# Masked copies of K in halves, in a linear ReLU attention kernel

## The chip, the cores and the metric

One core of a Trainium2 chip. The metric is the device time of one execution in microseconds (us); the kernel before was timed three times, and the profile is of one more execution. TensorE multiplies matrices, VectorE, ScalarE and GpSimd (POOL in the profile) work element by element, SyncE (SP) only issues DMAs here. PE, DVE and ACT in the profile are TensorE, VectorE and ScalarE.

## The reference

```python
# Q, K, V: float32 of shape (8, 12, 512, 64): batch, heads, rows, dim
Q_feat = np.maximum(0, Q)
K_feat = np.maximum(0, K)
KV = np.einsum('bhkd,bhkv->bhdv', K_feat, V)
K_sum = np.sum(K_feat, axis=2)
numerator = np.einsum('bhqd,bhdv->bhqv', Q_feat, KV)
denominator = np.einsum('bhqd,bhd->bhq', Q_feat, K_sum)
return numerator / (denominator[:, :, :, None] + 1e-10)
```

Attention without a softmax: for each of the 96 heads a 64 x 64 product `KV` of K and V over the 512 rows is made first, and then each row of Q is multiplied with it and divided by its own sum.

## The kernel before

The 96 heads are worked on in 12 octets of 8 heads (NO = 12). An octet of Q, K or V is 128 partitions of 32 rows of 64 numbers; a head lies in 16 partitions. POOL loads them with DMAs that turn float32 into bf16 (`load_q`, line 174, and `load`, line 179); the K and V of octet 0 come as float32 over SP. Nine octets fit in the input buffers (NI = 9), so the loads run far ahead of the work.

All 64 partitions of four heads are multiplied in one matmul, so the heads have to be kept apart by zeros. VectorE therefore makes two masked copies of K, `kf[:, :, s, :]` for s = 0 and 1 (`prep_k`, line 189): relu of K, times a mask that keeps every second head. V has two masked copies in `vo` (`prep_v`, line 195), with a column of ones that gives `K_sum`.

The code runs in steps (`step`, line 313). Step i does the following on each engine, in this order:

- TensorE (`products`, line 350, a loop that waits on semaphores): transposes Q of octet i (line 360); makes KV in two groups of 64 matmuls in all, group 0 over rows 0 to 15 and group 1 over rows 16 to 31 of each partition, with a signal after each group (line 369); transposes the result of octet i-1 back to rows (line 378); multiplies Q with KV, first the denominators, then two halves of the numerators (all line 354, into `ps_kv` and `ps_x`).
- ScalarE: relu of the transposed Q (line 209), KV out of PSUM (line 217), half of a V copy for octet i+1 (line 200), the numerators out of PSUM (line 225).
- VectorE: a copy of Q of octet i+1 (`copy_q`, line 206), the two K copies of octet i+1 (line 191), two `norm`s of octet i-1 (numerator times reciprocal into the output buffer, line 242), three small instructions for the denominators of octet i (lines 230 to 237), and the rest of the V copies of octet i+1 (line 202).

The tile `kf` exists once. So the K copies of octet i+1 have to wait until TensorE has read those of octet i. The class `Order` (line 9) derives such waits from keys: each operation lists the keys it reads and writes, and it waits for the operations of other engines that last used them. The engines take their instructions strictly in the order written. TensorE's side is entered by `do.looped`, whose keys for the two KV groups are the lists `KF[0]` and `KF[1]` (line 257).

Three queues set the order of transfers. POOL's DMAs go over six semaphores in turn, so that each waits for the landing of the one six places before it; POOL also issues the stores of octets 0 and 1 (line 251). SP issues the stores of octets 2 to 11 (line 254), and each of them also waits for the K load of octet 11 to have landed. The output has seven buffers (NOUT = 7, two of which held octet 0's K and V first): octet o's `norm` writes buffer (o + 2) mod 7 and waits for the store of octet o-7.

Of the kernel before, what the change touches and what calls it, by code (L numbers as in the profile page):

```python
# [96 lines left out]
def kernel(  # L97
# [14 lines left out]
    R = S * 4 // P  # L112
# [24 lines left out]
    mask = sb.tile([P, 2, 2], fp32, name="mask")  # L137
    mask_h = sb.tile([P, 8, 2], fp32, name="mask_h")
    kf = sb.tile([P, RQ, 2, D], bf16, name="kf")
    vo = sb.tile([P, RQ, 2, D4], bf16, name="vo")  # L140
# [26 lines left out]
    do = Order(nc, sems)  # L167

    def kv_src(o):
        if o == 0:  # L170
            return (o_sb[0], ("o", 0)), (o_sb[1], ("o", 1))
        return [(x[o % NI].rearrange("p (r d) -> p r d", d=D), (n, o % NI)) for n, x in (("k", k_sb), ("v", v_sb))]
# [6 lines left out]
    def load(o):  # L179
        i = o % NI  # L180
        for n, X, t in (("K", Kr, k_sb), ("V", Vr, v_sb)):
            if n == "V" and o == NO - 1:
                load_q(o)
            do.op("pool", lambda e: e.dma_start(out=t[i], in_=X[o], single_packet=True), writes=[(n.lower(), i)],  # L184
                  dma=lane("pool"))
        if o < NO - 1:
            load_q(o)

    def prep_k(o, s):
        src, key = kv_src(o)[0]  # L190
        do.op("dve", lambda e: e.tensor_scalar(kf[:, :, s, :], src, scalar1=0.0, scalar2=mask[:, 0, s:s + 1],  # L191
                                               op0=Alu.max, op1=Alu.mult),
              reads=[key, ("mask", 0)], writes=[("kf", s)])

    def prep_v(o, t, halves, who, sem=None):
        src, key = kv_src(o)[1]
        rs = slice(R * halves[0], R * halves[-1] + R)
        to, src, m = vo[:, rs, t, 2:D + 2], src[:, rs], mask[:, 1, t:t + 1]
        if who == "act":
            make = lambda e: e.activation(to, src, Act.Copy, scale=m)  # L200
        else:
            make = lambda e: e.tensor_scalar(to, src, scalar1=m, scalar2=None, op0=Alu.mult)  # L202
        do.op(who, make, reads=[key, ("mask", 1), "vo1"], writes=[("vo", t, j) for j in halves], sem=sem)

    def copy_q(o):
        do.op("dve", lambda e: e.tensor_copy(q2, q_sb[o % NI]), reads=[("q", o % NI)], writes=["q2"], sem="q2")  # L206

    def relu_q(j):
        do.op("act", lambda e: e.activation(qt[:, j * (U // 2):(j + 1) * (U // 2)], ps_qt[j], Act.Relu),  # L209
              reads=[("pq", j)], writes=[("qt", j)])  # L210
# [3 lines left out]
    def evac_kv():  # L214
        for s in range(2):
            for c in range(2):
                do.op("act", lambda e: e.copy(  # L217
                    kvd[64 * c:64 * c + 64, s:8:2, c * D1:c * D1 + D1].rearrange("p (g t) d -> p g t d", t=2),
                    ps_kv[64 * s:64 * s + 64, :, 0:2 * (D + 2)].rearrange(
                        "p g (t d) -> p g t d", t=2)[:, :, :, c:c + D1]),  # L220
                    reads=[("pk", 0), ("pk", 1)], writes=[("kvd", s, c)], sem="ev" if s + c == 2 else None)

    def copy_ot(j, who):
        to, src = ot[:, :, 4 * j:4 * j + 4], ps_x[j].rearrange("p (h u c) -> p u h c", h=4, u=U)
        do.op(who, lambda e: e.copy(to, src) if who == "act" else e.tensor_copy(to, src),  # L225
              reads=[("x", j)], writes=[("ot", j)], sem=f"t{j}")

    def denominators():
        ps = ps_den.rearrange("p (u h c) -> p u (h c)", u=U, h=8)
        do.op("dve", lambda e: e.scalar_tensor_tensor(  # L230
            own.rearrange("p u h c -> p u (h c)"), ps, 1e-10,
            mask_h.rearrange("p h c -> p (h c)").unsqueeze(1).to_broadcast([P, U, 16]), op0=Alu.add, op1=Alu.mult),
            reads=["pd", "mask_h"], writes=["own"])
        do.op("dve", lambda e: e.tensor_reduce(  # L234
            out=den.rearrange("p (u c) -> p u c", c=2), in_=own.rearrange("p u h c -> p u c h"), op=Alu.add,
            axis=mybir.AxisListType.X), reads=["own"], writes=["den"])
        do.op("dve", lambda e: e.reciprocal(rec, den), reads=["den"], writes=["rec"])

    def norm(o, j):
        i = (o + 2) % NOUT  # L240
        rs = slice(16 * j, 16 * j + 16)
        do.op("dve", lambda e: e.tensor_tensor(o_sb[i][:, rs], ps_x[j].rearrange("p (r d) -> p r d", d=D),  # L242
                                               rec[:, rs].unsqueeze(2).to_broadcast([P, 16, D]), op=Alu.mult),
              reads=[("x", j), "rec"], writes=[("o", i, j)] if i > 1 else [("o", i, j), ("o", i)], sem=f"n{j}")

    def store(o):
        i = (o + 2) % NOUT
        to, src = Or[o], o_sb[i].rearrange("p r d -> p (r d)")
        keys = [("o", i, h) for h in range(2)]
        if o + AHEAD + 1 < NO:  # L250
            do.op("pool", lambda e: e.dma_start(out=to, in_=src, single_packet=True), reads=keys, dma=lane("pool"))
        else:
            keys.append(("k", (NO - 1) % NI))
            do.op("sp", lambda e: e.dma_start(out=to, in_=src), reads=keys,
                  dma=lane("sp" if o + NOUT < NO else "last"), kept=o + NOUT >= NO)

    KF = [[("kf", 0), ("kf", 1), ("vo", 0, j), ("vo", 1, j), "vo1"] for j in range(2)]
    PK = [("pk", 0), ("pk", 1)]
    QT = [("qt", 0), ("qt", 1)]
    OT = [("ot", 0), ("ot", 1)]  # L260
# [31 lines left out]
    def setup():  # L292
        do.op("dve", lambda e: e.tensor_copy(ident32, ident), reads=["ident"], writes=["ident32"])
        for c in range(2):
            do.op("dve", lambda e: e.tensor_reduce(
                out=mask_h[:, :, c], in_=ident32.rearrange("p (h b) -> p h b", h=8), op=Alu.add,
                axis=mybir.AxisListType.X), reads=["ident32"], writes=[("mh", c), "mask_h"])
        do.op("dve", lambda e: e.tensor_reduce(
            out=mask[:, 0, :], in_=mask_h[:, :, 0].rearrange("p (a s) -> p s a", s=2), op=Alu.add,
            axis=mybir.AxisListType.X), reads=["mask_h"], writes=[("mask", 0)])  # L300
        prep_k(0, 0)
        prep_k(0, 1)
        prep_v(0, 1, (0,), "act", "a0")
        prep_v(0, 0, (0, 1), "dve", "d0")
        prep_v(0, 1, (1,), "dve", "d1")
        do.op("dve", lambda e: e.memset(kvf.bitcast(fp32)[:, 0:4 * D1], 0.0), writes=KVD, sem="n0")
        do.op("dve", lambda e: e.memset(kvf.bitcast(fp32)[:, 4 * D1:], 0.0), writes=KVD, sem="n1")
        copy_q(0)
        for j in range(2):
            nc.scalar.sem_inc(sems[f"t{j}"], 1)  # L310
            do.note("act", "act", (), (), f"t{j}", 1)

    def step(i):
        r = i + 1
        more, last = i + 1 < NO, i == NO

        if not last:
            do.looped([("q2", r)], ["q2", "ident"], [("pq", 0)])
            do.looped([], ["q2", "ident"], [("pq", 1)])
            relu_q(0)  # L320
            relu_q(1)
            do.looped([("a0", r), ("d0", r)], KF[0], PK + ["pd"])
            do.looped([("d1", r)], KF[1], PK + ["pd"])
            evac_kv()
            if more:
                prep_v(i + 1, 1, (0,), "act", "a0")
                copy_q(i + 1)
                prep_k(i + 1, 0)
                prep_k(i + 1, 1)
        if i > 0:  # L330
            o = i - 1
            do.looped([("t0", r), ("t1", r)], [*OT, "ident32"], [("x", 0)])
            do.looped([], [*OT, "ident32"], [("x", 1)])
            for j in range(2):
                norm(o, j)
            store(o)
            if o + AHEAD + 1 < NO:
                load(o + AHEAD + 1)
        if not last:
            do.looped([("ev", r)], [*QT, *KVD], ["pd"])  # L340
            denominators()
            for j in range(2):
                do.looped([(f"n{j}", r)], [*QT, *KVD], [("x", j)])
            copy_ot(0, "act")
            copy_ot(1, "act" if more else "dve")
            if more:
                prep_v(i + 1, 0, (0, 1), "dve", "d0")
                prep_v(i + 1, 1, (1,), "dve", "d1")
# [85 lines left out]
```

## Time and profile before

| | us |
|---|---|
| three runs, median (lowest to highest) | 125.53 (125.38 to 125.61) |
| profiled execution | 125.56 |
| its span, first to last instruction | 123.7 |
| TensorE matmuls busy | 85.0 (69%) |
| VectorE busy | 82.4 (67%) |
| ScalarE busy | 78.3 (63%) |
| DMAs on the chain that ended last | 71% |
| VectorE's K copies of octets 1 to 11 (22) | 15.6, 0.75 each |

Spans and starts in the profile are counted from the first instruction; the execution's time has 1.86 us more than the span. "Idle before" in a profile line tells how long the engine stood still before the instruction, and the name behind the arrow what it waited for last. The granted clock is that of TensorE, 1.00 being full speed. The chain that ended last is found by going back from the last instruction to whatever released it. Two instructions of one engine can overlap at their ends, so a pair may take less than the sum of its two times.

### The profile page before, as it was taken

To read this page: it belongs to the slowest core of one execution; us is meant where nothing else is said; L and a number is where in the kernel's file an instruction comes from. 1 tells how busy PE (TensorE), PEld (TensorE's weight loads), DVE (VectorE), ACT (ScalarE), POOL (GpSimd) and SP (SyncE) were. 2 spreads that over 40 slices of the span, in tenths; PEclk is the share of its full clock that TensorE was granted. 3 is DMA by queue.
4 is the path that set the end of the run, shared out by engine and by line. 5 is a ranking of instruction groups with operands and counts; after the bars stand their busy time and mean duration, and the time that the engine had idled before them with its cause. 6 is when DMAs were issued, how large, how long until landed. Compare 5 with 4: busy or idle time off the path is not lost.

```text
span 123.7 us, 3402 instructions
## 1 busy us (share of the span) xinstructions
PE 85.0 (69%) x1440; PEld 73.5 (59%) x1440; DVE 82.4 (67%) x127; ACT 78.3 (63%) x108; POOL 27.6 (22%) x55
## 2 busy tenths in 40 slices
PE   0000097697896979969799697996978918983900
PEld 0000096686794867949589485794856916972900
DVE  1261904769789697895987959869688649067330
ACT  0000762998987889878898788987869736652000
POOL 5795311331131213312421142221000000000000
PEclk9999999999999999999999999999999996897555
DMA  3999999999999999999999999999999999999955
GB/s 69 404 315 222 213 215 212 212 212 212 216 215 215 212 212 212 217 215 213 213 215 212 212 212 267 334 215 234 354 217 212 404 424 432 421 421 429 434 238 212
DMA packets 6916, 32.55 MB, mean 263 GB/s; under 512 B 768, under 2 KB 768, under 8 KB 5120
## 3 DMA queue, kind: packets, MB, share of 16 engines
q0 software_dynamic: 5184, 19.93, 75.8%
q1 hardware_dynamic: 1728, 12.58, 24.7%
q14 instruction: 3, 0.02, 0.0%
q8 instruction: 1, 0.02, 0.0%
HBM read 37.75 MB, written 12.58 MB: 407 GB/s over the span
## 4 chain that ended last, share of the span: by engine, by line
DMA 71%; PE 8%; DVE 7%; issue 5%; POOL 4%; POOLq 0%; DVEq 0%; SPq 0%
DMA k_sb<-in_K_dram 54%; DMA q_sb<-in_Q_dram 12%; DMA out_dram<-o_sb 6%; DVE o_sb L242 5%; PE ps_x L378 4%; PE ps_kv L369 2%; POOL vo L263 2%; PE ps_qt L360 1%; DVE ot_sb L225 1%; PE ps_x L354 1%; POOL k_sb L184 1%; POOL mask L263 1%; POOL q_sb L175 1%; POOL v_sb L184 0%; DVE den L234 0%
## 5 line engine op out<-in xcount | busy, mean ns | idle before, releaser
L242 DVE TENSOR_TENSOR o_sb<-ps_x,rec 128x1024 f32<-128x1024 f32 x24 | 28.5, 1217 | 9.2 <-PE ps_x L378 6.6
L225 ACT COPY ot_sb<-ps_x 128x1024 f32<-128x1024 f32 x23 | 23.2, 1013 | 10.7 <-PE ps_x L354 9.8
L369 PE MATMUL ps_kv<-vo,kf 64*128 64x132 bf16 x768 | 26.7, 228 | 0.8 <-DVE vo L202 0.2
L378 PE MATMUL ps_x<-ident,ot_sb 128*128 128x128 f32 x192 | 25.3, 288 | 1.7 <-DVE ot_sb L225 1.7
L369 PEld LDWEIGHTS ps_kv<-vo,kf 64*128 64x128 bf16 x768 | 24.7, 99 | 2.6 <-issue 2.6
L360 PE MATMUL ps_qt<-ident,q 128*128 128x128 bf16 x192 | 14.4, 235 | 16.4 <-DVE q L206 15.4
L209 ACT ACTIVATE qt<-ps_qt 128x1024 bf16<-128x1024 bf16 x24 | 23.4, 1031 | 1.9 <-PE ps_qt L360 1.9
L378 PEld LDWEIGHTS ps_x<-ident,ot_sb 128*128 128x128 f32 x192 | 22.3, 148 | 3.2 <-issue 2.0
L360 PEld LDWEIGHTS ps_qt<-ident,q 128*128 128x128 bf16 x192 | 12.4, 106 | 19.0 <-DVE q L206 15.4
L217 ACT CAST kvd<-ps_kv 64x260 bf16<-64x260 f32 x48 | 17.9, 374 | 8.5 <-PE ps_kv L369 7.6
L354 PE MATMUL ps_x<-qt,kvd 128*128 128x256 bf16 x96 | 14.9, 281 | 12.1 <-DVE o_sb L242 12.0
L191 DVE TENSOR_SCALAR kf<-k_sb,mask 128x2048 bf16<-128x2048 bf16 x22 | 15.6, 750 | 8.5 <-PE ps_kv L369 8.4
L354 PEld LDWEIGHTS ps_x<-qt,kvd 128*128 128x128 bf16 x96 | 7.7, 100 | 16.9 <-DVE o_sb L242 16.3
L206 DVE COPY q<-q_sb 128x2048 bf16<-128x2048 bf16 x12 | 8.2, 686 | 8.6 <-DMA q_sb<-in_Q_dram 8.6
L175 POOL DMA_DIRECT2D q_sb<-in_Q_dram x12 | 9.2, 763 | 19.0 <-DMA q_sb<-in_Q_dram 14.6
L200 ACT ACTIVATE vo<-v_sb,mask 128x1024 bf16<-128x1024 bf16 x11 | 12.7, 1153 | 0.6 <-DMA v_sb<-in_V_dram 0.4
L202 DVE TENSOR_SCALAR vo<-v_sb,mask 128x2048 bf16<-128x2048 bf16 (+1 forms) x22 | 11.6, 568 | 0.0
L184 POOL DMA_DIRECT2D k_sb<-in_K_dram x11 | 7.7, 697 | 16.8 <-DMA k_sb<-in_K_dram 12.9
L184 POOL DMA_DIRECT2D v_sb<-in_V_dram x11 | 6.3, 576 | 16.5 <-DMA v_sb<-in_V_dram 12.7
L200 ACT ACT_TABLE_LOAD x1 | 1.3, 1283 | 12.2 <-DMA o_sb<-in_V_dram 12.2
L354 PE MATMUL ps_kv<-kvd,qt 128*128 128x16 bf16 x192 | 6.9, 179 | 1.7 <-ACT kvd L217 1.7
L354 PEld LDWEIGHTS ps_kv<-kvd,qt 128*128 128x128 bf16 x192 | 6.4, 96 | 2.0 <-ACT kvd L217 1.9
(21 smaller groups left out, 27.6 us busy)
## 6 DMA issues: line engine op xcount, KB each, us to landing
out_dram<-o_sb SPq DMA_DIRECT2D x10, 1024.0 KB, 12.4
q_sb<-in_Q_dram POOLq DMA_DIRECT2D x12, 512.0 KB, 14.5
k_sb<-in_K_dram POOLq DMA_DIRECT2D x11, 512.0 KB, 14.4
v_sb<-in_V_dram POOLq DMA_DIRECT2D x11, 512.0 KB, 14.4
out_dram<-o_sb POOLq DMA_DIRECT2D x2, 1024.0 KB, 14.7
o_sb<-in_K_dram SPq DMA_DIRECT2D x1, 1024.0 KB, 6.2
o_sb<-in_V_dram SPq DMA_DIRECT2D x1, 1024.0 KB, 10.7
```

What stands on the lines that cost most here:

```text
L184: do.op("pool", lambda e: e.dma_start(out=t[i], in_=X[o], single_packet=True), writes=[(n.lower(), i)], dma=lane("pool"))
L191: do.op("dve", lambda e: e.tensor_scalar(kf[:, :, s, :], src, scalar1=0.0, scalar2=mask[:, 0, s:s + 1], op0=Alu.max, op1=Alu.mult), reads= ...
L200: make = lambda e: e.activation(to, src, Act.Copy, scale=m)
L202: make = lambda e: e.tensor_scalar(to, src, scalar1=m, scalar2=None, op0=Alu.mult)
L209: do.op("act", lambda e: e.activation(qt[:, j * (U // 2):(j + 1) * (U // 2)], ps_qt[j], Act.Relu), reads=[("pq", j)], writes=[("qt", j)])
L217: do.op("act", lambda e: e.copy(kvd[64 * c:64 * c + 64, s:8:2, c * D1:c * D1 + D1].rearrange("p (g t) d -> p g t d", t=2), ps_kv[64 * s:64 ...
L225: do.op(who, lambda e: e.copy(to, src) if who == "act" else e.tensor_copy(to, src), reads=[("x", j)], writes=[("ot", j)], sem=f"t{j}")
L242: do.op("dve", lambda e: e.tensor_tensor(o_sb[i][:, rs], ps_x[j].rearrange("p (r d) -> p r d", d=D), rec[:, rs].unsqueeze(2).to_broadcast( ...
L354: return pe.matmul(out_, lhsT, rhs, start=True, stop=True, skip_group_check=True)
L360: x = pe.transpose(ps_qt[u // 8][:, u % 8, :], q2[:, u, :], ident)
L369: x = pe.matmul(ps_kv[:, h, 0:2 * (D + 2)].rearrange("p (t d) -> p t d", t=2), kf[ps, R * g + k, :, :].rearrange("p s d -> p (s d)"), vo[p ...
L378: x = pe.transpose(ps_x[u // 8][:, u % 8 * P:u % 8 * P + P], ot[:, u].rearrange("p h c -> p (h c)"), ident32)
```

## The change

`prep_k` gets a third argument, the halves of the rows that it copies, and writes one key for each half. The KV groups of TensorE read only their own half's keys. For octet 0 both halves are still copied by one instruction for each s. In the steps, the two instructions of 32 rows become four of 16 rows: first both masked copies of rows 0 to 15, which wait for TensorE's group 0 of the octet before, then both of rows 16 to 31, which wait for group 1. `copy_q` stays ahead of all four and the `norm`s stay behind them.

```diff
-    def prep_k(o, s):
+    def prep_k(o, s, halves):
         src, key = kv_src(o)[0]
-        do.op("dve", lambda e: e.tensor_scalar(kf[:, :, s, :], src, scalar1=0.0, scalar2=mask[:, 0, s:s + 1],
+        rs = slice(R * halves[0], R * halves[-1] + R)
+        do.op("dve", lambda e: e.tensor_scalar(kf[:, rs, s, :], src[:, rs], scalar1=0.0, scalar2=mask[:, 0, s:s + 1],
                                                op0=Alu.max, op1=Alu.mult),
-              reads=[key, ("mask", 0)], writes=[("kf", s)])
+              reads=[key, ("mask", 0)], writes=[("kf", s, j) for j in halves])
...
-    KF = [[("kf", 0), ("kf", 1), ("vo", 0, j), ("vo", 1, j), "vo1"] for j in range(2)]
+    KF = [[("kf", 0, j), ("kf", 1, j), ("vo", 0, j), ("vo", 1, j), "vo1"] for j in range(2)]
...
-        prep_k(0, 0)
-        prep_k(0, 1)
+        prep_k(0, 0, (0, 1))
+        prep_k(0, 1, (0, 1))
...
                 copy_q(i + 1)
-                prep_k(i + 1, 0)
-                prep_k(i + 1, 1)
+                for j in range(2):
+                    for s in range(2):
+                        prep_k(i + 1, s, (j,))
```

## The prediction

> **What bounds the kernel now.** I read the chain that ended last first, then the timeline around it, then the clock in stretches of 3.41 us. The chain (start, length, what):
>
> ```profile
> 63.69 14.43 DMA q_sb<-in_Q_dram
> ...
> 78.40 14.85 DMA k_sb<-in_K_dram
> ...
> 93.27 7.43 DMA out_dram<-o_sb
> ...
> 100.72 2.37 DVE o_sb L242 x2
> ...
> 117.68 1.23 DVE o_sb L242
> ```
>
> It goes over transfers until 100.70: each load waits for the one six places ahead of it, the K load of octet 11 lands at 93.25, the store of octet 2, which waits for that landing, ends 7.43 us after, and its end frees the output buffer of the `norm` of octet 9. From there engines carry the chain. The page's slice row has the DMA engines at 9 of 10 or more from the second slice to the thirty-eighth. What VectorE does before 100.72 matters only if it is late for one of these landings. So: how late is it?
>
> ```profile
> 71.45 2.07 PE L369 MATMUL ps_kv<-vo,kf 64*128 64x132 bf16 x64
> 71.62 0.69 DVE L206 COPY q<-q_sb 128x2048 bf16<-128x2048 bf16 x1
> ...
> 73.45 1.97 PE L378 MATMUL ps_x<-ident,ot_sb 128*128 128x128 f32 x16
> ...
> 73.56 1.42 DVE L191 TENSOR_SCALAR kf<-k_sb,mask 128x2048 bf16<-128x2048 bf16 x2 [1.25 <-PE ps_kv L369]
> 74.89 2.47 DVE L242 TENSOR_TENSOR o_sb<-ps_x,rec 128x1024 f32<-128x1024 f32 x2
> ...
> 88.42 0.69 DVE L206 COPY q<-q_sb 128x2048 bf16<-128x2048 bf16 x1 [1.23 <-DMA q_sb<-in_Q_dram]
> ...
> 90.84 2.36 DVE L242 TENSOR_TENSOR o_sb<-ps_x,rec 128x1024 f32<-128x1024 f32 x2 [0.37 <-DMA out_dram<-o_sb]
> ```
>
> The first five lines are an ordinary step (octet 8's KV product): the `kf` copies start 1.25 us late, 0.11 after the transpose back (L378) starts, since they wait for the second KV group, and the `norm` follows. The last two are where loads catch up: `copy_q` of octet 10 waits 1.23 us for Q, the `norm` of octet 8 waits 0.37 for the store of octet 1. One step later the `norm` of octet 9 waits 2.11:
>
> ```profile
> 100.72 2.35 DVE L242 TENSOR_TENSOR o_sb<-ps_x,rec 128x1024 f32<-128x1024 f32 x2 [2.11 <-DMA out_dram<-o_sb]
> ...
> 102.00 0.61 PE L354 MATMUL ps_x<-qt,kvd 128*128 128x256 bf16 x4 [2.54 <-DVE o_sb L242]
> ...
> 103.97 1.91 PE L360 MATMUL ps_qt<-ident,q 128*128 128x128 bf16 x16
> ...
> 105.81 2.30 PE L369 MATMUL ps_kv<-vo,kf 64*128 64x132 bf16 x64
> ```
>
> Those 2.11 us are the slack of everything ahead of it. Behind it TensorE is cold: L360 takes 1.91 here against 1.06 in an ordinary step. Stretches (us, PE, PEld, DVE, ACT, POOL busy, granted clock, DMA share, GB/s):
>
> ```profile
> 75.64:79.05 3.41, 2.30 (x32) 1.60 (x28) 3.31 (x7) 2.66 (x4) 1.18 (x2) 1.00 1.03 362
> ...
> 99.53:102.94 3.41, 0.61 (x4) 0.31 (x4) 2.22 (x2) 1.06 (x2) 0.00 (x0) 1.00 1.01 428
> 102.94:106.35 3.41, 3.21 (x32) 2.72 (x34) 2.21 (x6) 2.87 (x4) 0.00 (x0) 0.50 1.00 423
> 109.77:113.18 3.41, 1.88 (x27) 1.17 (x24) 3.34 (x6) 1.01 (x1) 0.00 (x0) 1.00 1.00 423
> ...
> 21.03:24.44 3.41, 1.82 (x34) 1.73 (x35) 2.51 (x6) 3.29 (x6) 0.68 (x2) 1.00 1.05 211
> ```
>
> TensorE had been idle 2.53 us (99.47 to 102.00); the clock falls to 0.50 at 102.94, returns at 106.35, 3.41 us on, and falls again at 113.18, 6.83 after that. So it steps on a grid of 3.41 us: a cell with 0.61 us of work and one with 1.88 are followed by a slow one, cells with 1.82 and 2.30 are not. The limit lies near 1.8.
>
> **The change, by parts.** The profiled execution took 125.56 us, 123.7 of it span and 1.86 around it; the median is 125.53.
>
> 1. *Two more VectorE instructions an octet.* No row shows a half K copy. Its nearest rows:
>
> ```profile
> L191 DVE TENSOR_SCALAR kf<-k_sb,mask 128x2048 bf16<-128x2048 bf16 x22 | 15.6, 750 | 8.5 <-PE ps_kv L369 8.4
> ...
> L202 DVE TENSOR_SCALAR vo<-v_sb,mask 128x2048 bf16<-128x2048 bf16 x11 | 7.2, 657 | 0.0
> ...
> L202 DVE TENSOR_SCALAR vo<-v_sb,mask 128x1024 bf16<-128x1024 bf16 x11 | 5.3, 478 | 0.0
> ```
>
> Half of V costs 0.478/0.657 = 0.73 of the whole; on K's 0.75 that is 0.55, and since two in a row overlap by 0.08 (a pair takes 1.42, not 1.50), 0.47 from start to start. Bounds: 0.34 (half of the whole's 0.67) and 0.67 (no cheaper). I take 0.47, by the V row, its likest. An octet's copies then cost 4 x 0.47 + 0.08 = 1.96 instead of 1.42: +0.54 us (bounds 0.02 and 1.34).
>
> 2. *The first pair moves forward.* Times from the start of L369: group 0 ends at +1.03, `copy_q` at +0.85, group 1 at +2.07. The first pair runs from +1.05 to +1.99, in the 1.25 us gap, which covers its 0.94. The second starts at +2.10 and lets the `norm` start at +3.04; today that is +3.44 (71.45 to 74.89). Next late is TensorE's L378: with VectorE waiting, the `norm` of octet 10 started 1.20 after L378 did (108.04 to 109.24), so +3.20. Gain 0.24 us a step, a period of 7.44 to 7.57 instead of 7.68 to 7.81. Even at 0.34 it stays 0.24; at 0.67 the `norm` starts at +1.05 + 4 x 0.67 = +3.73, 0.29 later than now.
>
> 3. *The new wait.* The first half waits for group 0. Behind it in VectorE's order stand the other halves, two `norm`s, three denominator instructions, the V copies; TensorE and ScalarE wait for the `norm`s. Group 0 ends a microsecond before group 1, so it holds nothing that did not wait longer before. Where Q comes late, all four halves follow `copy_q`: with `copy_q` w later than +0.16 the `norm` can start at +0.78 + w + 1.88, past +3.20 when w is over 0.54. Loads bring an octet in 7.36 us, so the faster loop runs into that and then goes at the loads' pace.
>
> 4. *Queues.* POOL's loads wait for landings (its wait rows name only DMAs and the start), K of octet 11 goes into a buffer read long before, SP's ten stores wait for the K landing. No DMA is added or moved.
>
> *Sum up to 100.72.* The loop is shorter from octet 4 on, so L369 of octet 9 starts about 0.9 to 1.7 us before its 86.94. There it ends: Q of octet 10 is still copied at 88.42. Four halves from 89.04 end at 90.92 plus a tail, so the `norm` of octet 8 starts at 90.92, not 90.84: +0.08 (0 at 0.34 each, +0.88 at 0.67). That is absorbed in 2.11. Gain at 100.72: zero.
>
> *What the early work does to the clock.* L378 of step 9 then ends near 89.2 to 90.0 and the small matmuls near 89.6 to 90.4, so TensorE idles 1.7 to 2.5 us until 92.1. The cell 89.29 to 92.70 holds some 0.9 to 1.7 us of work instead of 2.61, under the limit, so I expect a slow cell from 92.70 to 96.11 that the kernel lacks now. Its price, from the same instructions at 103 to 106: L354 1.04 for 0.61, L360 1.91 for 1.06; L369 of octet 10 starts 0.8 to 1.3 us after its 95.09. L378 then starts at 98.0 to 98.4, its first half is ready 1.20 later, at 99.2 to 99.6, and `kf` of octet 11 is done by 99.5: all before 100.72. Cover left is 1.1 us. The cell 99.53 to 102.94 then has 1.4 to 1.8 us of TensorE work in place of 0.61, still at or under the 1.88 that did not suffice, so it is followed by the same slow cell, and the tail is today's.
>
> Forecast: 125.56 + 0 = 125.56 for that execution, 125.5 for a median. Within 0.2% (0.25 us) is what a measurement here cannot tell from no change.
>
> The Trainium skill, TensorE: Matmul & The Clock Gate, "What's actually happening", says that the activity window is about 3.4 us, free-running, and not reset by a kernel's start. The grid of 3.41 us agrees. By it, the cells would lie elsewhere in another execution, and the faster rival below would come in some executions; four executions between 125.38 and 125.61 don't show such a spread.
>
> **Rivals.**
>
> *Faster: the tail stays warm.* If the work pushed behind 99.53 brings the cell over the limit, the slow cell at 102.94 goes. For it: 1.82 once sufficed and the estimate reaches 1.8. Against: 1.88 did not. Price: (1.04 - 0.61) + (1.91 - 1.06) + (2.30 - 2.07) = 1.51 us off the chain. The stores keep the DMA engines full until 118.2, and the last store moves its data from about 119.4, so only 1.2 comes out: 124.3.
>
> *Slower: VectorE's extra copies hold up POOL's descriptors.* POOL's DMA instructions take 0.53 us mostly, but 0.83 to 1.02 beside VectorE copies (1.02 at 48.92, ahead of a `copy_q` at 49.13). 22 more copies in other places can stretch more of them. Should each of the six reissues on the chain (14.54, 29.25, 44.03, 58.74, 63.69, 78.40) land 0.1 to 0.49 later, K of octet 11 is 0.6 to 2.9 late, and so is all behind it: 126.1 to 128.4, at the nearer end 126.1. Against: the reissues with 0.53 and with 0.93 landed alike in 14.43, since five more loads are under way. It decides once the DMA share falls below 1 between 16 and 93 us.
> The Trainium skill, SBUF — State Buffer, the warning on the "DVE blocks DMA" trap, speaks for this rival: a DMA issued from GpSimd has its descriptors written there, and a VectorE copy in a two-port mode locks it out. The long issues agree; that the engines then stand idle no row here shows.
>
> *Slower: halves as dear as wholes.* At 0.67 each the period grows by 0.29, the `norm` of octet 9 comes at about 100.7, just at its limit; at 0.75 without overlap it would be about 2 us late, less up to 1.51 for a warmer tail: 126.1. Against: the V row.
>
> *The change does not do what it says:* the halves still start after group 1. Then the `norm` starts at +2.10 + 1.88, 0.54 later each step: 3.2 over six steps and 1.1 over the next two, less the 0.46 that the `norm` of octet 8 has in hand (86.94 + 3.44 against 90.84) and the 2.11, so 1.75 late, less up to 1.51 for a warm tail: 125.8 to 127.3. Against: the key of each half is written apart, and group 0 signals by itself.
>
> **How the numbers follow.** Forecast 0.54 (within 0.2%). Warm tail 0.25 (faster). POOL's descriptors 0.13, dear halves 0.05, no overlap 0.03 (slower: 0.21). The likeliest is 125.5, by itself 125.3 to 125.75. The range goes to the warm tail below, 124.2, and takes in the near ends of the slower cases above, 126.2; the far ends are left out, about 1 in 10.
>
> **What would show it.** Right: 44 half copies near 0.55 us, the first pair ahead of L378, steps of 7.4 to 7.6 in the middle, Q still copied near 88.4 and the `norm` of octet 9 still at 100.7 with a wait of 1.5 us or more, a slow cell around 92.7 to 96.1. Wrong: that wait gone (loop too slow), the K landing away from 93.25 (transfers), or L360 of octet 11 near 1.06 instead of 1.91 (warm tail).

## The result, and the profile after

| | time, median of 22 runs (us) | lowest to highest |
|---|---|---|
| before | 125.44 | 125.27 to 125.92 |
| after | 125.83 | 125.48 to 126.37 |

The ratio is 1.0030, with a 95% interval of 1.0019 to 1.0041: the change makes the kernel 0.39 us slower. The forecast was no change, 125.5; 125.83 lies in its range, but the move is clear of the noise and I had called it the least likely side.

The profiled execution after the change took 126.16 us, 124.2 of it span. Line numbers are shifted by one or two: `norm` is L243 now, the K copies L192, the KV groups L371, the transpose back L380, the transpose of Q L362. The chain that ended last (start, length, what) has the same links as before:

```profile
6.03 8.46 DMA k_sb<-in_K_dram
...
63.92 14.53 DMA q_sb<-in_Q_dram
...
78.74 14.77 DMA k_sb<-in_K_dram
...
93.53 7.43 DMA out_dram<-o_sb
...
100.98 2.37 DVE o_sb L243 x2
...
118.11 1.23 DVE o_sb L243
```

The timeline of step 8 and of the two places where loads catch up, and the K copies by shape:

```profile
77.84 2.07 PE L371 MATMUL ps_kv<-vo,kf 64*128 64x132 bf16 x64
78.55 0.69 DVE L207 COPY q<-q_sb 128x2048 bf16<-128x2048 bf16 x1 [0.46 <-DMA q_sb<-in_Q_dram]
...
79.16 1.68 DVE L192 TENSOR_SCALAR kf<-k_sb,mask 128x1024 bf16<-128x1024 bf16 x4
...
79.84 1.97 PE L380 MATMUL ps_x<-ident,ot_sb 128*128 128x128 f32 x16
...
81.04 2.35 DVE L243 TENSOR_TENSOR o_sb<-ps_x,rec 128x1024 f32<-128x1024 f32 x2 [0.21 <-PE ps_x L380]
...
88.67 0.70 DVE L207 COPY q<-q_sb 128x2048 bf16<-128x2048 bf16 x1 [3.14 <-DMA q_sb<-in_Q_dram]
...
91.13 2.36 DVE L243 TENSOR_TENSOR o_sb<-ps_x,rec 128x1024 f32<-128x1024 f32 x2 [0.18 <-DMA out_dram<-o_sb]
...
94.25 1.78 PE L362 MATMUL ps_qt<-ident,q 128*128 128x128 bf16 x16
...
100.98 2.36 DVE L243 TENSOR_TENSOR o_sb<-ps_x,rec 128x1024 f32<-128x1024 f32 x2 [1.18 <-DMA out_dram<-o_sb]
```

```profile
L192 DVE TENSOR_SCALAR kf<-k_sb,mask 128x1024 bf16<-128x1024 bf16 x44 | 18.5, 481 | 1.3 <-PE ps_kv L371 1.2
```

In step 8 the four halves run from 79.16 to 80.84, begun after a `copy_q` that waited for Q, and the `norm` starts at 81.04, 1.20 us after L380. The loop now waits for the loads: `copy_q` sat idle for Q for 13.2 us in the whole execution, where it was 8.6. For octet 10 it waits 3.14 us (1.23 before), and still starts at 88.67. The `norm` of octet 8 waits 0.18 us for its store, the `norm` of octet 9 waits 1.18 and starts at 100.98. So the step that the change speeds up is faster, and nothing of it gets past the loads.

Stretches of TensorE's clock after the change (columns as in the prediction; a slow cell is a stretch of 3.41 us at a granted clock of 0.50):

```profile
91.00:94.41 3.41, 1.38 (x11) 0.79 (x12) 3.21 (x5) 1.23 (x2) 0.00 (x0) 1.00 1.07 214
94.41:97.83 3.42, 3.42 (x52) 3.22 (x52) 1.91 (x4) 2.74 (x3) 0.00 (x0) 0.50 1.05 311
101.24:104.65 3.41, 1.73 (x17) 1.14 (x18) 3.34 (x6) 2.04 (x3) 0.00 (x0) 1.00 1.01 428
104.65:108.06 3.41, 3.41 (x58) 3.21 (x57) 0.82 (x2) 2.25 (x3) 0.00 (x0) 0.50 1.01 425
```

The slow cell before step 10 is there, 94.41 to 97.83, and L362 of octet 10 takes 1.78 us. The next slow cell is at 104.65, not 102.94.

For this pair of executions the chain accounts for the difference in the span. It begins with the first load on the chain and reaches SP's ten stores (start of the first issue, time to the end of the last). The kernel before, then after the change, whose first load stands above:

```profile
6.03 8.22 DMA k_sb<-in_K_dram
...
93.27 26.00 SPq L254 DMA_DIRECT2D out_dram<-o_sb  x10
```

```profile
93.53 26.16 SPq L255 DMA_DIRECT2D out_dram<-o_sb  x10
```

The first K load lands at 14.49 instead of 14.25, before the first half copy runs (20.00), and K of octet 11 at 93.51 instead of 93.25. The `norm` of octet 9 starts 0.26 later, the last `norm` 0.43 later (118.11 and 117.68; the slow cells lie elsewhere between the two), the last store is issued at 119.36 instead of 118.94, and the span is 124.2 instead of 123.7. One pair of executions can't say what of this is due to the change. The time outside the span differs too: 126.16 - 124.2 = 1.96 against 125.56 - 123.7 = 1.86. That one I had taken for a constant.

Every run has its own span, so the time outside it can be taken run by run. The 22 runs after the change have 2.02 us of it on average and a span of 123.84; of the 22 runs before, these spans are not known, but 35 runs of the kernel before in the next group of runs have 1.81 and 123.63. That splits the loss into about 0.2 outside and 0.2 in the span, and each half needed its own test.

### The profile page after: what moved, and what is told of

It reads as the page before. It is cut to its first block, busy times and chain, and to the rows that moved or that the text cites. A ratio compares the mean times of both kernels' runs of the same rounds, so it can differ in the third digit from the quotient of the medians.

```text
span 124.2 us, 3424 instructions
## 1 busy us (share of the span) xinstructions
PE 87.2 (70%) x1440; PEld 75.5 (61%) x1440; DVE 85.3 (69%) x149; ACT 78.6 (63%) x108; POOL 25.1 (20%) x55
## 4 chain that ended last, share of the span: by engine, by line
DMA 71%; PE 8%; DVE 7%; issue 6%; POOL 4%; POOLq 0%; DVEq 0%; SPq 0%
DMA k_sb<-in_K_dram 54%; DMA q_sb<-in_Q_dram 12%; DMA out_dram<-o_sb 6%; DVE o_sb L243 5%; PE ps_x L380 4%; PE ps_kv L371 3%; POOL vo L264 2%; PE ps_qt L362 1%; DVE ot_sb L226 1%; POOL mask L264 1%; POOL q_sb L175 1%; PE ps_x L356 0%; POOL k_sb L184 0%; POOL v_sb L184 0%; DVE den L235 0%
## 5 line engine op out<-in xcount | busy, mean ns | idle before, releaser
L243 DVE TENSOR_TENSOR o_sb<-ps_x,rec 128x1024 f32<-128x1024 f32 x24 | 28.5, 1220 | 8.5 <-PE ps_x L380 7.0
L371 PE MATMUL ps_kv<-vo,kf 64*128 64x132 bf16 x768 | 27.7, 233 | 0.4
L362 PE MATMUL ps_qt<-ident,q 128*128 128x128 bf16 x192 | 15.5, 245 | 16.8 <-DVE q L207 15.7
L371 PEld LDWEIGHTS ps_kv<-vo,kf 64*128 64x128 bf16 x768 | 25.8, 102 | 2.3 <-issue 2.3
L380 PE MATMUL ps_x<-ident,ot_sb 128*128 128x128 f32 x192 | 25.1, 287 | 1.7 <-DVE ot_sb L226 1.7
L362 PEld LDWEIGHTS ps_qt<-ident,q 128*128 128x128 bf16 x192 | 13.3, 111 | 19.7 <-DVE q L207 15.7
L380 PEld LDWEIGHTS ps_x<-ident,ot_sb 128*128 128x128 f32 x192 | 22.1, 146 | 3.2 <-issue 2.0
L192 DVE TENSOR_SCALAR kf<-k_sb,mask 128x1024 bf16<-128x1024 bf16 x44 | 18.5, 481 | 1.3 <-PE ps_kv L371 1.2
L207 DVE COPY q<-q_sb 128x2048 bf16<-128x2048 bf16 x12 | 8.3, 689 | 13.6 <-DMA q_sb<-in_Q_dram 13.2
L175 POOL DMA_DIRECT2D q_sb<-in_Q_dram x12 | 7.1, 589 | 20.1 <-DMA q_sb<-in_Q_dram 15.4
L184 POOL DMA_DIRECT2D k_sb<-in_K_dram x11 | 7.1, 644 | 17.3 <-DMA k_sb<-in_K_dram 13.4
```

The source lines that it names most:

```text
L192: do.op("dve", lambda e: e.tensor_scalar(kf[:, rs, s, :], src[:, rs], scalar1=0.0, scalar2=mask[:, 0, s:s + 1], op0=Alu.max, op1=Alu.mult) ...
L362: x = pe.transpose(ps_qt[u // 8][:, u % 8, :], q2[:, u, :], ident)
L371: x = pe.matmul(ps_kv[:, h, 0:2 * (D + 2)].rearrange("p (t d) -> p t d", t=2), kf[ps, R * g + k, :, :].rearrange("p s d -> p (s d)"), vo[p ...
L380: x = pe.transpose(ps_x[u // 8][:, u % 8 * P:u % 8 * P + P], ot[:, u].rearrange("p h c -> p (h c)"), ident32)
```

## The experiments

The runs come in four groups, each on one chip, with 35 runs of the kernel before beside the others. "Added" counts VectorE instructions beyond those of the kernel before; "outside" is the mean of time minus span over the runs. The span of a single run is known to 0.1 us; the standard error of a mean is 0.03 to 0.14 for the span and at most 0.03 for outside.

| kernel | added | time, median | ratio (95%) | span | outside |
|---|---|---|---|---|---|
| before, group 1 | 0 | 125.44 | | 123.63 | 1.81 |
| e1 changed kernel | 22 | 125.67 | 1.0018 (1.0003 to 1.0032) | 123.69 | 1.96 |
| e2 halves for octets 1 to 9 | 18 | 125.86 | 1.0035 (1.0019 to 1.0050) | 123.70 | 2.19 |
| e3 halves for octets 10, 11 | 4 | 125.46 | 1.0002 (0.9990 to 1.0014) | 123.65 | 1.83 |
| e4 changed, step 9 filled | 22 | 125.59 | 1.0015 (1.0003 to 1.0027) | 123.65 | 1.95 |
| before, group 2 | 0 | 125.43 | | 123.65 | 1.81 |
| e5 before + 22 memsets | 22 | 125.54 | 1.0014 (1.0000 to 1.0027) | 123.62 | 1.98 |
| e6 before + 18 memsets | 18 | 125.87 | 1.0035 (1.0022 to 1.0049) | 123.72 | 2.18 |
| e7 before, tail filled | 0 | 125.77 | 1.0031 (1.0012 to 1.0049) | 124.03 | 1.82 |
| e8 changed, steps 9 to 11 filled | 22 | 125.80 | 1.0028 (1.0015 to 1.0041) | 123.87 | 2.00 |
| before, group 3 | 0 | 125.56 | | 123.78 | 1.81 |
| e9 changed + 8 memsets | 30 | 125.51 | 0.9992 (0.9978 to 1.0006) | 123.74 | 1.81 |
| e10 changed + 20 memsets | 42 | 125.52 | 0.9994 (0.9975 to 1.0014) | 123.75 | 1.83 |
| e11 e4 + 20 memsets | 42 | 125.73 | 1.0023 (0.9998 to 1.0047) | 124.11 | 1.82 |
| e12 before + 42 memsets | 42 | 125.44 | 0.9991 (0.9975 to 1.0006) | 123.71 | 1.80 |
| before, group 4 | 0 | 125.48 | | 123.72 | 1.81 |
| e13 changed kernel | 22 | 125.68 | 1.0022 (1.0009 to 1.0034) | 123.73 | 2.03 |
| e14 changed + 8 memsets | 30 | 125.57 | 1.0011 (0.9995 to 1.0027) | 123.80 | 1.81 |
| e15 before + 26 memsets | 26 | 125.70 | 1.0014 (0.9998 to 1.0030) | 123.88 | 1.82 |
| e16 before + 12 memsets | 12 | 125.63 | 1.0016 (1.0001 to 1.0031) | 123.84 | 1.81 |

### Which octets, and the clock: e1 to e4

My first theory, A, was the clock: the idle stretch in step 9 makes a slow cell, which pushes the tail's slow cell onto work. Its rivals were B, the last two octets' extra VectorE work, and C, a later load stream.

e1 is the changed kernel again. e2 and e3 split only some octets:

```diff
-                for j in range(2):
+                for hs in (((0,), (1,)) if i + 1 < 10 else ((0, 1),)):      # e2; e3 has >= 10
                     for s in range(2):
-                        prep_k(i + 1, s, (j,))
+                        prep_k(i + 1, s, hs)
```

e4 keeps TensorE busy in step 9 with 20 fillers, products that nobody reads and that go to an unused part of PSUM:

```diff
                 x.then_inc(sems["pe"], 1)
+                with pe.If(r > 9), pe.If(r < 11):
+                    for _ in range(20):
+                        mm(ps_kv[:, 0, 256:512], qt[:, 0, :], kvf[:, 0:256])
                 q = qt.rearrange("p u (h c) -> p u h c", h=8)
```

> The changed kernel once more, for a second profile. Measured so far: 1.003 times the kernel before, +0.39 us; in its profile K of octet 11 landed at 93.51 (before 93.25), the norm of octet 9 began at 100.98 (100.72), norm of octet 10 at 109.88 (109.24), so 8.90 us between the two instead of 8.52. Theory A (clock): TensorE's idle stretch in step 9 (2.75 us instead of 0.80) and the slow cell after it push step 10's TensorE work later, and the slow cell of the tail then falls on the KV groups of octet 11 instead of on idle time: again +0.3 to +0.4, norm 9 to norm 10 about 8.9 on average, more spread than before. Theory C (loads): the load stream ends 0.25 later because of the change: K of octet 11 again at 93.5. If it lands at 93.25 in this profile, that difference was of one execution.

> K copies in halves for octets 1 to 9 only; octets 10 and 11 in whole copies as before. Theory A: the loop is early and TensorE idles in step 9 as in the changed kernel, so 1.003 (+0.3 to +0.4 us). Theory B (the extra VectorE work of the last two octets, four halves behind the late copy of Q): back at the time before, 1.000. Theory C (22 more instructions delay the load stream in proportion): +0.3.

> K copies in halves for octets 10 and 11 only; octets 1 to 9 as before. Theory A: the loop is not early, TensorE idles about 0.8 us in step 9, no slow cell there: 1.000 (within 0.1 us). Theory B: 1.003. Theory C: about 1.0005.

> The changed kernel, with 20 matmuls of 128x256 into an unused part of PSUM in step 9 only, between the denominators and the wait for the norm of octet 8, so that TensorE is busy for some 2.2 us of the 2.75 it idles there. Theory A: no slow cell before step 10, L360 of octet 10 back from 1.78 to 1.06, the tail as in the kernel before, ratio back to 1.000 (0 to +0.1 us). Theories B and C: still 1.003.

By their times alone, e2 (+0.42) and e3 (+0.02) fit theory A and rule out B. The split into span and outside says otherwise: e2's span is 0.07 above the kernel before, and its loss is 0.38 outside the span, more than that of the changed kernel, with fewer halves. Theory A has no place for that. C falls too: K of octet 11 lands at 92.99 in e1, before the 93.25 of the kernel before, so 93.51 was of one execution.

e1 and e4, the same stretch of the timeline, first e1:

```profile
90.57 2.36 DVE L243 TENSOR_TENSOR o_sb<-ps_x,rec 128x1024 f32<-128x1024 f32 x2
...
93.69 1.88 PE L362 MATMUL ps_qt<-ident,q 128*128 128x128 bf16 x16
...
100.43 2.36 DVE L243 TENSOR_TENSOR o_sb<-ps_x,rec 128x1024 f32<-128x1024 f32 x2 [1.21 <-DMA out_dram<-o_sb]
```

```profile
88.96 2.77 PE L356 MATMUL ps_kv<-kvd,qt 128*128 128x16 bf16 x36
...
93.83 1.06 PE L362 MATMUL ps_qt<-ident,q 128*128 128x128 bf16 x16
...
100.58 2.36 DVE L243 TENSOR_TENSOR o_sb<-ps_x,rec 128x1024 f32<-128x1024 f32 x2 [2.63 <-DMA out_dram<-o_sb]
```

In e4 the filling works (16 products for the denominators and 20 fillers in 2.77 us, L362 of octet 10 back at 1.06), in e1 the slow cell is there (1.88), and both have the `norm` of octet 9 wait for its store, at 100.43 and 100.58. The slow cell exists, as predicted, and costs nothing there. e4 still loses 0.15, of which 0.14 is outside.

e2's profile adds something that I had wrong. Its tail was warm (TensorE at full clock) up to the `norm`s of octet 11:

```profile
114.53 2.35 DVE L243 TENSOR_TENSOR o_sb<-ps_x,rec 128x1024 f32<-128x1024 f32 x2 [1.32 <-PE ps_x L380]
116.91 0.33 SPq L255 DMA_DIRECT2D out_dram<-o_sb  x1
```

Its last store was issued at 116.91, two us before the kernel before issued its own (118.9), and its span is 123.7 all the same. The profiles of e4, e5, e6, e8 and e10 also have the last store issued by 117.4, and spans of 123.5 to 124.4. At the end of such a span the DMA engines run nearly empty; this is e6, last store issued at 116.18:

```profile
120.00:121.00 1.00, 0.00 (x0) 0.00 (x0) 0.00 (x0) 0.00 (x0) 0.00 (x0) 0.50 0.82 344
121.00:122.00 1.00, 0.00 (x0) 0.00 (x0) 0.00 (x0) 0.00 (x0) 0.00 (x0) 0.50 0.12 49
```

A later issue does count. In the seven profiles with a last store issued from 118.87 to 119.70 the span ends 4.8 to 4.9 us after it: 118.94 and 123.7 before, 119.36 and 124.2 after the change.

### A longer program and a warm tail: e5 to e8

If the number of VectorE's instructions sets the time outside the span, instructions that do nothing must cost as much. e5 and e6 are the kernel before, with whole copies, and 22 or 18 small memsets of an added tile, `spare`, ahead of the first K copy, where VectorE waits for K anyway (shown for e5):

```diff
+        for z in range(22):
+            memset("dve", spare[:, z:z + 1], 0.0, ("spare", z))
         prep_k(0, 0)
```

e7 and e8 keep TensorE busy in the idle stretches of the last steps: the block of e4 with 18 matmuls, for step 10 in the kernel before and for steps 9 and 10 in the changed one, and 14 more behind the last product of step 11.

> The kernel before, whole K copies, with 22 memsets of one column of a spare tile on VectorE, put into its idle time at the start (4.1 to 7.2 us), so as many more instructions as the change has. Seen so far, as means over the runs: time outside the span 1.81 us before, 2.02 and 1.96 for the changed kernel, 2.19 with halves for octets 1 to 9, 1.83 with halves for octets 10 and 11 alone, so half of the loss lies outside the span. Theory D (the number of instructions sets the time outside the span): outside 1.95 to 2.2, span unchanged at 123.6, time +0.15 to +0.4. Theory E (the halves themselves, through what they do at the end): outside 1.81, time unchanged.

> The same with 18 memsets, the number that halves for octets 1 to 9 add. Theory D: outside 1.95 to 2.2; if the number alone sets it, near 2.19 and above that with 22. Theory E: 1.81.

> The kernel before with TensorE kept busy in its idle stretches of the tail: 18 matmuls of 128x256 into an unused part of PSUM in step 10 after the denominators, 14 after the last product of step 11. No slow cell in the tail: last norm ends near 116.3 instead of 118.9. By the prediction's faster rival the execution is then 1.2 us shorter, 124.3. Theory F (the transfers end as late whatever the engines do; two profiles with a warm tail and a last norm at 116.3 and 116.9 had spans of 123.6 and 123.7): span 123.5 to 123.7, time 125.3 to 125.5.

> The changed kernel with the same 18 matmuls in steps 9 and 10 and 14 after step 11. Theory A (a slow cell that falls later costs the changed kernel 0.1 to 0.2 of span): span back to that of the kernel before, 123.6, spread no wider; time outside the span stays near 2.0, so +0.15 to +0.2 us in all. If the span stays at 123.7 to 123.85, the clock is not the cause of that part.

e5 and e6 reproduce the odd numbers: 1.98 with 22 memsets, 2.18 with 18, beside 1.95 to 2.03 and 2.19 with as many instructions from halves. Outside the span the number of VectorE's instructions decides, not what they are. Instructions added to TensorE don't show there: with 20 or 32 matmuls more in its program, e4, e7 and e8 have 1.95, 1.82 and 2.00, beside 1.96 (e1), 1.81 (before) and 2.02 (the first runs after the change). The transfers after the last store, from 122.5 us on in 40 slices, show a difference. Before, then after the change, then e5:

```profile
GB/s 0 0 0 0 0 0 0 0 0 0 0 0 0 0 0 0 0 0 0 0 0 0 0 0 0 0 0 0 0 0 0 0 0 0 0 0 0 0 0 0
DMA packets 0, 0.00 MB, mean 0 GB/s; under 512 B 0, under 2 KB 0, under 8 KB 0
```

```profile
GB/s 0 0 0 0 0 0 0 0 0 0 0 0 0 0 0 0 0 0 0 0 0 0 0 0 0 60 0 0 0 0 0 0 0 0 0 0 0 0 0 0
...
q14 instruction: 1, 0.01, 0.5%
```

```profile
GB/s 0 0 0 0 0 0 0 0 0 0 0 0 0 0 0 0 0 0 0 0 60 0 0 0 0 0 0 0 0 0 0 0 0 0 0 0 0 0 0 0
DMA packets 1, 0.01 MB, mean 1 GB/s; under 512 B 0, under 2 KB 0, under 8 KB 0
...
q14 instruction: 1, 0.01, 0.5%
```

Before, nothing moves. After, and in e5, one packet of 8 KB of the queue that loads instructions comes at about 125.9 and 125.3, after the last data of the last store (122.8 and 122.2) and after the last instruction of the span. All six profiles with 22 added instructions have it, 1.8 to 2.0 us after the end of the span (the expectations of e9 and e15 count this from the last store's data by mistake); none of those with 0, 4, 12 or 18 do, though outside is largest with 18. An earlier packet of that queue moves with the memsets at the start, from 52.3 us in the kernel before to 45.0 with 12, 38.0 with 18, 30.6 with 26 and 22.9 with 42, while two others stay near 54 and near 107. So I read the moving ones as VectorE's program.

e7 missed its aim. Its steps are longer, 8.0 us from one KV product to the next (73.54 to 81.50) where the kernel before takes 7.7 to 7.8: TensorE stands still for about 0.4 us ahead of the transposes of Q, where the second added branch is. A slow cell, 88.45 to 91.86, then falls on the KV product of octet 9. This is its timeline:

```profile
80.50 1.06 PE L360 MATMUL ps_qt<-ident,q 128*128 128x128 bf16 x16 [0.37 <-issue]
81.50 2.07 PE L369 MATMUL ps_kv<-vo,kf 64*128 64x132 bf16 x64
...
90.18 2.83 PE L369 MATMUL ps_kv<-vo,kf 64*128 64x132 bf16 x64
...
102.22 2.35 DVE L242 TENSOR_TENSOR o_sb<-ps_x,rec 128x1024 f32<-128x1024 f32 x2
```

The `norm` of octet 9 starts at 102.22 and no longer waits for a store. So e7 says nothing on a warm tail. e8 does better: the `norm` of octet 9 waits for its store at 100.80, TensorE stays at full clock from 27.4 to 119.6, the last `norm` ends at 116.66, and the span is not shorter (123.87 on average, 123.65 before). So a warm tail gains nothing. The expectation for theory A was 123.6, and 123.7 to 123.85 if the clock is not the cause; 123.87 speaks against the clock, but since e8 has the branches that made e7's steps longer, it does not exclude it.

### Past the block: e9 to e12

If VectorE's program is loaded in blocks and the cost comes from a last block that is loaded too late (theory D1), a longer program, which needs that block earlier, should be free again. Then the changed kernel gets faster by instructions that do nothing.

> The changed kernel with 8 memsets of one column on VectorE in its idle time at the start: 30 instructions more than the kernel before. Time outside the span so far by the number of added VectorE instructions: 1.81 (0), 1.83 (4), 2.18 and 2.19 (18), 1.98, 1.96 and 2.02 (22). All kernels with 22 show a fetch of 8 KB of instructions 1.7 to 1.9 us after the last store's data, the others none. Theory D1 (a block of VectorE's program that is fetched at the end; the later the place in the block, the earlier the fetch): outside 1.80 to 1.95 with 30, falling. Theory D2 (any longer program costs): 2.0 or more. Span as in the changed kernel, 123.7 to 123.85.

> The changed kernel with 20 such memsets: 42 instructions more than the kernel before. Theory D1: outside back to 1.81, so the changed kernel gets 0.2 us faster by 20 instructions that do nothing, 125.5 to 125.65. Theory D2: 2.0 or more. Span 123.7 to 123.85, if the other part of the loss is in the halves; 123.65 if that part was chance.

> The changed kernel with those 20 memsets and with the 20 filling matmuls in step 9 (no slow cell before step 10; it had a span of 123.65 before). Theories A and D1 together: outside 1.81, span 123.65, the time of the kernel before, 1.000. If the span is above 123.75 here too, the slow cell is not what lengthens it.

> The kernel before, whole K copies, with 42 memsets at the start. Theory D1: outside 1.81, span 123.65, time 1.000. Theory D2: outside 2.0 or more.

D1 holds in all four: outside is 1.80 to 1.83 with 30 and with 42 instructions added. The changed kernel with 8 memsets more runs at 0.9992 of the kernel before (0.9978 to 1.0006). Its transfers from 116 us and from 122.5 us on:

```profile
GB/s 437 437 437 410 410 437 410 328 137 82 55 437 437 437 437 437 437 437 437 55 0 0 0 0 0 0 0 0 0 0 0 0 0 0 0 0 0 0 0 0
...
q14 instruction: 1, 0.01, 0.2%
```

```profile
GB/s 0 0 0 0 0 0 0 0 0 0 0 0 0 0 0 0 0 0 0 0 0 0 0 0 0 0 0 0 0 0 0 0 0 0 0 0 0 0 0 0
DMA packets 0, 0.00 MB, mean 0 GB/s; under 512 B 0, under 2 KB 0, under 8 KB 0
```

One instruction packet of 8 KB is now loaded before the last store is through (at 118.9), and none after it. With 42 there are two instruction loads in the stretch from 95 us on as well, the earlier of them at 102 to 103 us. e11 has the fetch out of the way too (1.82); its span of 124.11, with a standard error of 0.14, is the highest of all, so filling step 9 does not help. The mean hides two groups: seven runs at 123.5 to 123.9 with a mean granted clock of 0.952 or more, and five at 124.4 to 124.8 with 0.946 or less. The profiled run is one of the five. It has no slow cell before step 10, but K of octet 11 lands at 94.00 there, later than in any other profile where the chain goes over it, and it has slow cells in the tail. So the slow cell before step 10 is not what makes these runs long; whether late loads or the clock of the tail do, one profile can't tell.

### The span, and the edges: e13 to e16

> The changed kernel again, for its span beside that of the kernel before on one chip. If the halves lengthen the span (theory A or any other in the span): span +0.15 to +0.2 us over the kernel before. If only the instruction fetch costs: span within 0.1 of it, outside 1.95 to 2.05, time +0.15 to +0.25.

> The changed kernel with 8 memsets more, again. Only the fetch costs: outside 1.81, span within 0.1 of the kernel before, time within 0.1, and below the changed kernel of the same call by 0.15 to 0.25. If the span is lengthened by the halves: time +0.15 to +0.2.

> The kernel before with 26 memsets, between 22 (outside 1.98, fetch 1.8 us after the last store's data) and the 30 of the changed kernel with 8 (1.81, fetch before the last store's data). Theory D1: fetch at a time in between, outside 1.81 to 1.98.

> The kernel before with 12 memsets, between 4 (1.83) and 18 (2.18). Theory D1: no block is fetched at the end yet and outside is 1.81 to 1.85, or the fetch is already needed and it is 2.1 to 2.4; a value in between, near 2.0, would speak for a cost that grows with the number.

The span of the changed kernel is 123.73 beside 123.72 for the kernel before, and outside it takes 2.03 against 1.81: nearly all of its 0.23 us (means) lies outside here. With 8 memsets more, outside is back at 1.81 and the ratio 1.0011 has 1 in its interval; the median is 0.11 below the changed kernel's, less than the 0.15 to 0.25 expected, since its span is 0.07 higher. Outside is 1.81 at 12 and 1.82 at 26, so of the numbers tried only 18 and 22 cost. The ratio of e16 leaves 1 out of its interval although its outside time is that of the kernel before, by its span alone.

The packets that move fall in one order. The more instructions are added, the earlier the last of them comes (the one near 107 left aside): at 102 to 103 us with 42, at 118.9 with 30, 0.6 us after the end of the span with 26 (e15, as D1 expected), 1.8 to 2.0 after it with 22. With 18 it would come later still, past what the profile holds; that is how I read the highest cost without a packet, and no trace shows it. With 12 or fewer none seems to be needed.

The 0.2 us in the span of the first 22 runs did not come back. Kernels with halves in every octet and no filling stand 0.06 above, 0.04 below, 0.03 below, 0.01 above and 0.08 above the kernel before of their group. The kernel before with memsets alone stands between 0.07 below and 0.16 above (e12, e15), so differences of 0.1 to 0.2 in the span come and go with no cause that I can name. What made the first 22 runs longer stays open.

## Why the prediction was wrong

The step that failed is the last one of the sum, "125.56 + 0 = 125.56". It carried the 1.86 us around the span over as fixed, and part 1 priced the two instructions an octet by their durations alone; what a longer program costs was put at nothing without a reason. The runs show 0.14 to 0.22 us for it: with 22 instructions more on VectorE, 1.95 to 2.03 us lie outside the span, against 1.81. That the number of instructions is the cause is shown by e5, where memsets cost the same, and by e9 and e14, where more instructions take the cost away. How it comes about, a block of VectorE's program loaded after the end of the span, is argued from the packets.

This accounts for nearly all of the loss in e13, most of it in e1, and half of the 0.39 measured first. The other half was 0.2 us of span in the first 22 runs. The two repeats of the changed kernel are only 0.23 and 0.20 us slower in all (medians), so that half belongs to those runs and not to every execution of the change; its cause stays open.

Of the other steps:

- *A half K copy, 0.47 from start to start.* It is 0.40: four halves take 1.67, so an octet's copies cost 0.25 more, not 0.54. The row by itself is 0.481, close to the 0.478 of V's half; scaling by V's ratio was wrong, the half of V itself the better neighbour.
- *The first pair moves forward and the `norm` starts 1.20 after the transpose.* Right: 79.84 to 81.04. The loop then ran into the loads, as part 3 said.
- *Gain at 100.72: zero.* Right: the `norm` of octet 9 waits for its store in every profile with halves, at 100.40 to 100.98 where nothing is filled, with the K landing within 0.35 of 93.25.
- *A new slow cell before step 10.* Right in the changed kernel's profile and in e1 (L362 1.78 and 1.88), and its price is hidden, as worked out. But e13, the same kernel, has none there (L362 of octet 10 takes 1.06), and e9 has none either, while e16 with whole copies has one (1.82). So it is where the cells fall in an execution that decides, and not the early loop alone.
- *The same slow cell in the tail.* Its place differs: 102.94 before, 104.65 and 103.92 in two executions of the changed kernel. No limit near 1.8 us of work sorts the cells: those with 1.73 and 1.88 were followed by a slow one, the one with 1.82 was not. The Trainium skill, TensorE: Matmul & The Clock Gate, "What's actually happening", says that the window is free-running, and these places agree. I held against the rule that four executions had nearly one time; that was no evidence, for a reason that the next point gives.
- *Faster rival, 1.2 us for a warm tail.* Its price is wrong, also where its condition holds. e2's and e8's profiles have the last `norm` end at 116.9 and 116.7, against 118.9, and their spans are 123.7 and 124.4. The prediction let the last store start at about 119.4 on free DMA engines. By the packet times in the trace it starts at 119.77 in the kernel before, the store ahead of it ends only at 119.95, and the last data at 122.41; in e2, with the last store issued two us earlier, the latter two are 119.95 and 122.40. So an early tail gains nothing, and a late one costs: 0.42 us of later issue were 0.42 us of span in the profile after the change.
- *Slower rivals.* POOL's descriptors: the reissues on the chain took 0.53 to 0.62 after the change but for the first (0.96, as before), and K of octet 11 landed at 92.99 in e1 and 92.97 in e13; it is not the cause. Dear halves and no overlap: the rows rule them out.

## What to carry to other kernels

Take the time apart run by run before explaining a difference of a few tenths: what lies in the span can be found in the profile's chain, what lies outside cannot. When a change alters the number of instructions and the chain does not move, pad the program with instructions that do nothing, in the old kernel and in the new one, before blaming the edit. And a loop made faster under a stream of loads gained nothing here: the wait for Q took it all and grew from 8.6 to 13.2 us of VectorE's time.

## What the runs showed of the hardware

- Instructions are loaded in packets of 8 KB while the kernel runs; the times of some move with the number of VectorE's instructions. With 18 or 22 of them added, 0.14 to 0.38 us more lie outside the span; with 4, 12, 26, 30 or 42 at most 0.02. With 22 the last packet comes after the end of the span, with 30 before the last store is through. That the wait for this packet is the cost is my reading of the two together; the packet at 26 is late as well (about 0.6 us after the span's last instruction, beside 1.8 to 2.0 with 22) and costs nothing.
- TensorE's clock steps in cells of 3.41 us whose place differs between executions. Cells with 1.38 and 1.73 us of work were followed by a slow one in the changed kernel, as 1.88 was before.
- A tail that ends its work 2 us earlier did not end the kernel earlier: last stores issued at 116.9 and 118.9 gave the same span of 123.7, though the DMA engines ran nearly empty at the end of such a span (share 0.12 in e6). One issued at 119.36 gave 124.2. Why the last packets of the earlier stores take so long is not shown.
